# Small transposes and compression layers placed inside projections, output-weight lo's behind P scalings, boundary banks exchanged, in a two-layer hybrid decoder trunk

## Chip, cores and metric

One core of a Trainium2 chip (trn2). The metric is device time in microseconds (us) of one launch, shown as the median of several runs with the lowest and the highest.

## What is computed

The input x has 256 tokens of 1,024 values in float32. Two layers follow each other, each `x <- x + RMSNorm_post(mixer(RMSNorm_pre(x)))`. The first mixer is chunked gated linear attention (GLA). The second is sparse attention (NSA) with three branches per query: compressed, selected and window. Its input projection yields, beside q and a gate z, three pairs of keys and values:

```python
q, kc, vc, ks, vs, kw, vw, gl, z = jnp.split(p, splits, axis=-1)
kc, ks, kw = rope(kc), rope(ks), rope(kw)          # 4 groups x 64
kcmp = compress(kc, pe_k, ck_w1, ck_w2)            # silu(flat(blocks + pe) @ w1) @ w2
vcmp = compress(vc, pe_v, cv_w1, cv_w2)
o = sum over branches of gate * softmax(q k^T) v   # per branch
return (o * silu(z)) @ w_out
```

(The last lines are shortened from the reference.) A result is to be exact to float32, which decides how matrix products are done.

## The kernel before

**Products.** TensorE multiplies rounded float32. Each operand is split into a hi (ScalarE, line 190) and a lo, which is raw minus hi (line 196), made by GpSimd (POOL) or VectorE (DVE) according to a table `LOS`. `mm3` (line 210) then runs three matmuls: hi by hi, lo by hi, hi by lo. Weights come by DMA in units of two k rows (SP's queue, four raw buffers; a raw buffer is free again when hi and lo have been made from it).

**Projections.** `proj` (line 222) runs 8 steps of three matmuls for one token tile t (128 tokens) into one accumulator bank; tag acc has two banks, s three, t two, o one. `chain` (line 217) fixes the order of chained pieces on TensorE. What is not chained is placed by the compiler's scheduler, for each engine, by its own forecast; once placed, the order on an engine is fixed.

**The boundary between the layers.** `out_proj(t)` (line 340) finishes layer 0 for a token tile: two banks, one for each half of the 1,024 outputs. `residual` (line 263) evacuates them one after the other: ScalarE squares a bank, VectorE copies it (`yg`, line 276), then the new x is written (line 281). `pre_T` (line 298) transposes x into `hT`, four transposes to a bank, for each half c.

**The projections of layer 1.** In order: kc(0), ks(0), kc(1), ks(1), kw0(0), kw0(1), kw1(0), kw1(1), then q and z; the number in brackets is the token tile. Behind kc, ks and kw0 a chain follows: ScalarE evacuates values (`vs_sb`, line 859, or `dup`, line 845), VectorE rotates keys (`rope`, lines 823 and 825), GpSimd adds the two products twice over into `dup` (line 832), TensorE transposes `dup` four times (`dup_T`, line 839), and ScalarE and VectorE copy the result into `kcT` (lines 849 and 850) or split it into `kTh` and `kTl`. When both token tiles of kcT are there, VectorE makes eight `flat` additions (line 885), and `hidden(u)`, u from 0 to 3 (line 891), multiplies flat by a quarter of the compression weights. A 32-column transpose of `vecs` (line 815) makes vT, which flat wants. `spread` (line 328) sends the norms' factors over the partitions with two matmuls. None of these small pieces is chained.

**The units.** `unit(g, t)` is attention for group g and tile t: scores (line 1001), P by ScalarE's exponentials, coefficients cf on VectorE (line 1041), scalings of P on GpSimd (line 1045), transposes of P (line 1074), products with v (line 1088), and pcT (line 1096) for the compressed branch. Among the last units of tile 0 the output weights are loaded and split (`ch_o`, lines 1217 to 1219), in steps k of 0, 2, 4, 6 and halves n.

## Time and profile before

| | us |
|---|---|
| median of 3 runs | 304.07 (303.97 to 305.38) |
| profiled execution | 302.72 |
| its span in the profile | 300.8 |
| TensorE busy | 286.6 |
| VectorE busy | 215.3 |
| ScalarE busy | 181.5 |
| GpSimd busy | 167.0 |

The rows below come from the profiled execution; their times count from the start of its span. The share of the time outside the span is 302.72 less 300.8, that is 1.9. Engines are written PE (TensorE), DVE (VectorE), ACT (ScalarE), POOL (GpSimd) and SP (which issues DMAs) in rows.

### The profile page before, as it was taken

The numbers are of one execution on the slowest core, as the hardware profiler recorded it, in microseconds if no ns is written. First come the engines' busy times: TensorE is split into PE (matmuls) and PEld (weight loads), VectorE is DVE, ScalarE is ACT, GpSimd is POOL, SyncE is SP. The second block draws the span as 40 slices with busy tenths as digits, with TensorE's granted clock in tenths as the row PEclk, the third lists the DMA queues.
The fourth block names the chain that finished last, engine by engine and source line by source line (L and its number), as shares of the span: only waits on it lengthen the run. The fifth ranks groups of instructions, "written<-read, shape, count | busy, mean of one in ns | idle before, by whom it ended". The sixth has DMA issues, their size and how long they took to land.

```text
span 300.8 us, 5374 instructions
## 1 busy us (share of the span) xinstructions
PE 286.6 (95%) x1788; PEld 239.7 (80%) x1788; DVE 215.3 (72%) x556; ACT 181.5 (60%) x468; POOL 167.0 (56%) x184
## 2 busy tenths in 40 slices
PE   7999999999999999889979999999997999999991
PEld 7888999999998887668958676899994678676660
DVE  1779569846979877576893536799999858877423
ACT  4896788667754757435534405679967637657301
POOL 1496968984383252927545035897799434172200
PEclk9999999999999999999999999999997799999998
DMA  7997588105677334394745785576144000100001
GB/s 214 403 362 217 151 258 288 56 22 186 204 220 212 92 82 130 64 289 147 195 162 144 274 263 180 190 218 232 42 142 139 2 0 0 71 2 0 2 0 71
DMA packets 28301, 44.57 MB, mean 148 GB/s; under 512 B 2865, under 2 KB 12513, under 8 KB 28274
## 3 DMA queue, kind: packets, MB, share of 16 engines
q1 hardware_dynamic: 28242, 44.23, 46.6%
q8 instruction: 14, 0.23, 0.3%
q14 instruction: 13, 0.11, 0.1%
q10 hardware_dynamic: 32, 0.01, 0.0%
HBM read 43.18 MB, written 1.05 MB: 147 GB/s over the span
## 4 chain that ended last, share of the span: by engine, by line
PE 63%; DVE 13%; issue 9%; POOL 6%; ACT 4%; DMA 3%; SPq 0%; POOLq 0%; DVEq 0%; ACTq 0%
PE acc L211 11%; PE acc L213 11%; PE acc L212 11%; PE s L468 4%; POOL lo L196 3%; PE s L212 3%; PE s L211 3%; PE s L213 3%; DVE lo L196 3%; PE o L894 3%; PE t L1074 3%; PE o L1088 3%; PE s L1001 2%; ACT hi L190 2%; DMA raw<-in_gla_w_in_dram 1%
## 5 line engine op out<-in xcount | busy, mean ns | idle before, releaser
L196 POOL TENSOR_TENSOR lo<-raw,hi 128x512 fp32r<-128x512 f32 (+2 forms) x63 | 82.8, 1334 | 44.4 <-ACT hi L190 44.4
L190 ACT ACTIVATE hi<-raw 128x512 fp32r<-128x512 f32 (+2 forms) x120 | 64.2, 583 | 37.7 <-DMA raw<-in_nsa_w_in_dram 26.6
L196 DVE TENSOR_TENSOR lo<-raw,hi 128x512 fp32r<-128x512 f32 (+2 forms) x57 | 53.6, 963 | 13.4 <-ACT hi L190 13.3
L1045 POOL TENSOR_SCALAR P<-P,cf 128x128 f32<-128x128 f32 (+1 forms) x64 | 29.2, 475 | 30.2 <-DVE cf L1041 14.4
L211 PE MATMUL acc<-hT,hi 128*128 128x256 f32 x160 | 45.2, 283 | 0.1
L212 PE MATMUL acc<-hT,hi 128*128 128x256 f32 x160 | 44.8, 280 | 0.0
L213 PE MATMUL acc<-hT,lo 128*128 128x256 f32 x160 | 44.5, 281 | 0.0
L211 PE MATMUL acc<-hi,hT 128*128 128x512 f32 (+2 forms) x112 | 39.2, 350 | 1.2 <-DVE yg L276 0.8
L213 PE MATMUL acc<-hi,hT 128*128 128x512 f32 (+2 forms) x112 | 38.9, 347 | 0.0
L212 PE MATMUL acc<-lo,hT 128*128 128x512 f32 (+2 forms) x112 | 38.8, 346 | 0.0
L1008 ACT ACTIVATE P<-P,mn 128x128 f32<-128x128 f32 (+1 forms) x64 | 28.4, 445 | 7.2 <-DVE mn L1006 5.9
L211 PEld LDWEIGHTS acc<-hT,hi 128*128 128x128 f32 x160 | 30.1, 188 | 0.4 <-DVE zT L362 0.3
L212 PEld LDWEIGHTS acc<-hT,hi 128*128 128x128 f32 x160 | 30.1, 188 | 0.1
L213 PEld LDWEIGHTS acc<-hT,lo 128*128 128x128 f32 x160 | 29.8, 188 | 0.0
L211 PEld LDWEIGHTS acc<-hi,hT 128*128 128x128 f32 x112 | 21.1, 188 | 5.3 <-ACT yg L269 1.2
L1006 DVE CUSTOM_DVE_ANT_0 P<-s,c 128x128 f32<-128x128 f32 (+1 forms) x64 | 20.6, 347 | 5.3 <-PE s L1001 4.4
L213 PEld LDWEIGHTS acc<-hi,hT 128*128 128x128 f32 x112 | 21.1, 188 | 2.9 <-DVE hT L311 0.4
L212 PEld LDWEIGHTS acc<-lo,hT 128*128 128x128 f32 x112 | 21.1, 188 | 2.0
L1074 PE MATMUL t<-c,P 128*128 128x128 f32 x96 | 17.4, 296 | 2.0 <-ACT pcT L1096 1.9
L440 POOL TENSOR_TENSOR lo<-raw,hi 128x512 fp32r<-128x512 f32 (+1 forms) x9 | 12.3, 1388 | 9.9 <-ACT hi L436 9.8
L1074 PEld LDWEIGHTS t<-c,P 128*128 128x128 f32 x96 | 11.1, 147 | 7.3 <-issue 3.6
L832 POOL TENSOR_TENSOR dup<-rt,rt 128x512 f32<-128x512 f32 x6 | 8.9, 1487 | 11.2 <-DVE rt L825 5.7
(268 smaller groups left out, 676.2 us busy)
## 6 DMA issues: line engine op xcount, KB each, us to landing
raw<-in_nsa_w_in_dram SPq DMA_DIRECT2D x24, 512.0 KB, 4.5
raw<-in_gla_w_in_dram SPq DMA_DIRECT2D x12, 512.0 KB, 6.1
raw<-in_gla_w_out_dram SPq DMA_DIRECT2D x8, 512.0 KB, 4.3
raw<-in_nsa_w_out_dram SPq DMA_DIRECT2D x8, 512.0 KB, 4.2
raw<-in_nsa_w_in_dram SPq DMA_DIRECT2D x8, 280.0 KB, 8.4
raw<-in_gla_w_in_dram SPq DMA_DIRECT2D x6, 344.0 KB, 3.4
home<-in_gla_w_in_dram SPq DMA_DIRECT2D x4, 512.0 KB, 6.7
w<-in_nsa_ck_w_dram SPq DMA_DIRECT2D x4, 512.0 KB, 3.8
```

The source lines that it names most:

```text
L190: m = after(nc.scalar.activation(hi[:, j, :n], raw[:, j, :n], AF.Copy), prev)
L196: eng.tensor_sub(lo[:, j, :n], raw[:, j, :n], f(hi[:, j, :n]))
L211: m = nc.tensor.matmul(o, a[0], b[0], start=start, stop=False, **kw)
L212: nc.tensor.matmul(o, a[0], b[1], start=False, stop=False, **kw)
L213: return m, nc.tensor.matmul(o, a[1], b[0], start=False, stop=stop, **kw)
L440: line(e, eng.tensor_sub(lo[:, j, :n], raw[:, j, :n], f(hi[:, j, :n])))
L468: m = nc.tensor.matmul(o[t][:, :chunk.n], hT[i][:, k, t * P:(t + 1) * P], w[j], start=(k == b == 0), stop=(k == KT - 1 and b == 2))
L894: nc.tensor.matmul(hid_b[kv * 64:(kv + 1) * 64, :CHID], flat[:, j, kv].rearrange("p g c -> p (g c)"), w1[u * 2 + kv][:, j % 4, :], start=( ...
L1006: nc.vector.tensor_tensor_reduce(out=o, in0=src, in1=masks[br], op0=ALU.add, op1=ALU.min, scale=-0.125, scalar=3.0e38, accum_out=self.mn[: ...
L1008: nc.scalar.activation(o, o, AF.Exp, scale=-1.0, bias=self.mn[:, j:j + 1], accum_out=self.sm[:, j:j + 1])
L1045: nc.gpsimd.tensor_scalar(o, o, cf[:, i * 2 + br:i * 2 + br + 1], 1.0, op0=ALU.mult, op1=ALU.mult)
L1074: pe(nc.tensor.transpose(b[:, i * P:(i + 1) * P], self.Pt[i][:, c0:c0 + P], ident))
```

## The change

1. **Output weights.** GpSimd's lo's of the output weights with k of 4 and 6 are put behind the last scaling of unit (3, 0) by a dependence in order.
2. **Banks.** In `out_proj(1)` the first half goes to bank acc and the second to s; before, the first went to s and the second to acc.
3. **Small transposes.** `pre_T(1, c)` is chained between steps of ks(0), at k of 4 and 5. The kc(0) transposes and the one of vecs are chained between ks(0) and kc(1). Those of ks(0) are at step 3 of kc(1), those of kc(1) at step 3 of ks(1), those of ks(1) at step 3 of kw0(0). `dup` has three buffers instead of two.
4. **Compression.** hidden(u) is chained; hidden(0) stands behind kw1(0) and hidden(1) behind kw1(1).

```diff
@@ -182,7 +182,7 @@
                 self.raw.append(raw)
...
-        def split_unit(self, prev=None, pace=None):
+        def split_unit(self, prev=None, pace=None, pool_prev=None):
             n, raw = self.n, self.raw[len(self.u)]
...
@@ -193,13 +193,15 @@
                     if i >= 0:
...
                 eng = nc.gpsimd if len(self.u) * 2 + j in self.pool else nc.vector
-                eng.tensor_sub(lo[:, j, :n], raw[:, j, :n], f(hi[:, j, :n]))
+                x = eng.tensor_sub(lo[:, j, :n], raw[:, j, :n], f(hi[:, j, :n]))
+                if eng is nc.gpsimd:
+                    after(x, pool_prev)
             self.u.append((hi, lo))
...
-        def split(self, pace=None):
+        def split(self, pace=None, pool_prev=None):
             while len(self.u) < len(self.raw):
-                self.split_unit(pace=pace)
+                self.split_unit(pace=pace, pool_prev=pool_prev)
             return self
...
@@ -219,12 +221,15 @@
         after(first, last[0])
...
-    def proj(chunk, hT, t, tag="acc"):
+    def proj(chunk, hT, t, tag="acc", between={}):
...
         for k in range(KT):
+            if k in between:
+                chain(first, b)
+                between[k]()
             a, b = mm3(o[:, :chunk.n], [h[:, k, t * P:(t + 1) * P] for h in hT], chunk.part(k), k == 0, k == KT - 1)
-            first = a if k == 0 else first
+            first = a if k == 0 or k in between else first
             chunk.mm[t * KT + k] = a
...
@@ -300,7 +305,7 @@
         b = bank(tag)
...
             m = nc.tensor.transpose(b[:, k * P:(k + 1) * P], X[:, t, (c * 4 + k) * P:(c * 4 + k + 1) * P], ident)
-            if layer == t == 0:
+            if t == 1:
                 chain(m, m)
...
@@ -339,7 +344,7 @@
...
-        o = [bank("s"), bank("acc" if t else "s")]
+        o = [bank("acc" if t else "s"), bank("s")]
         steps = [(k, n) for k in range(4) for n in range(2)] + [(k, n) for n in range(2) for k in range(4, KT)]
...
@@ -773,10 +778,9 @@
     rs1 = []
...
         out_proj(t, ch_o, oT, gpost)
-        for c in range(2):
-            last_hi = pre_T(t, c, 1, hT, "t")
         if t == 0:
-            ks_after = last_hi
+            for c in range(2):
+                ks_after = pre_T(t, c, 1, hT, "t")
         rs1.append(rms(t)[0])
...
@@ -811,9 +815,6 @@
     flat = cp.tile([P, 16, 2, GROUPS, 16], F32, tag="flat", name="flat")
...
     vT = cp.tile([P, 32], F32, tag="vT", name="vT")
-    b = bank()
-    nc.tensor.transpose(b[:, :32], vecs, ident[:32, :32])
-    nc.vector.tensor_copy(vT, b[:, :32])
...
@@ -828,39 +829,52 @@
         if not twice:
...
             return a
-        r = cp.tile([P, nh, 2, DH], F32, tag="dup", name=nm("dup"), bufs=2)
+        r = cp.tile([P, nh, 2, DH], F32, tag="dup", name=nm("dup"), bufs=3)
         nc.gpsimd.tensor_add(r, *(y.unsqueeze(2).to_broadcast([P, nh, 2, DH]) for y in (a, b)))
...
-    def dup_T(r):
+    def dup_T(r, held=True):
...
         for g in range(GROUPS):
-            nc.tensor.transpose(b[:, g * P:(g + 1) * P], r[:, g].rearrange("p e d -> p (e d)"), ident)
+            m = nc.tensor.transpose(b[:, g * P:(g + 1) * P], r[:, g].rearrange("p e d -> p (e d)"), ident)
+            if held:
+                chain(m, m)
         return b
-    def kc_part(t):
-        o = proj(ch_kc, hT, t)
-        rv = cp.tile([P, GROUPS, 2, DH], F32, tag="dup", name=nm("dup"), bufs=2)
+    def kc_part(t, between={}):
+        o = proj(ch_kc, hT, t, between=between)
+        rv = cp.tile([P, GROUPS, 2, DH], F32, tag="dup", name=nm("dup"), bufs=3)
         nc.scalar.activation(rv, o[:, 256:512].rearrange("p (g d) -> p g d", d=DH).unsqueeze(2)
                              .to_broadcast([P, GROUPS, 2, DH]), AF.Copy, scale=rs1[t])
-        for kv, r in ((0, rope(o[:, :256], 4, t, True)), (1, rv)):
-            bv = dup_T(r).rearrange("p (g n two) -> p g n two", g=GROUPS, two=2)
-            nc.scalar.activation(kcT[:64, kv, :, t * 64:(t + 1) * 64], bv[:64, :, :, 0], AF.Copy)
-            nc.vector.tensor_copy(kcT[64:, kv, :, t * 64:(t + 1) * 64], bv[64:, :, :, 1])
-    def k_T(o, t, c0):
-        b = dup_T(rope(o[:, :256], 4, t, True)).rearrange("p (g n) -> p g n", g=GROUPS)
+        parts = ((0, rope(o[:, :256], 4, t, True)), (1, rv))
+        def rest():
+            for kv, r in parts:
+                bv = dup_T(r).rearrange("p (g n two) -> p g n two", g=GROUPS, two=2)
+                nc.scalar.activation(kcT[:64, kv, :, t * 64:(t + 1) * 64], bv[:64, :, :, 0], AF.Copy)
+                nc.vector.tensor_copy(kcT[64:, kv, :, t * 64:(t + 1) * 64], bv[64:, :, :, 1])
+        return rest
+    def k_T(r, c0, held):
+        b = dup_T(r, held).rearrange("p (g n) -> p g n", g=GROUPS)
         split_bank(b, kTh[:, :, c0:c0 + P], kTl[:, :, c0:c0 + P])
-    def ks_part(t):
-        o = proj(ch_ks, hT, t)
+    def ks_part(t, between={}):
+        o = proj(ch_ks, hT, t, between=between)
         nc.scalar.activation(vs_sb[:, t, :], o[:, 256:512], AF.Copy, scale=rs1[t])
-        k_T(o, t, (1 - t) * P)
-    kc_part(0)
-    ks_part(0)
+        r = rope(o[:, :256], 4, t, True)
+        return lambda: k_T(r, (1 - t) * P, True)
+    rest = kc_part(0)
+    ks_rest = ks_part(0, {4 + c: lambda c=c: pre_T(1, c, 1, hT, "t") for c in range(2)})
+    rest()
+    b = bank()
+    m = nc.tensor.transpose(b[:, :32], vecs, ident[:32, :32])
+    chain(m, m)
+    nc.vector.tensor_copy(vT, b[:, :32])
...
@@ -877,29 +891,29 @@
     ch_z = [Chunk(w_in, N_Z + p * 512, 512) for p in range(2)]
...
     ch_kw[0].load()
-    kc_part(1)
+    rest = kc_part(1, {3: ks_rest})
+    ks_rest = ks_part(1, {3: rest})
     for kv in range(2):
...
                                  vT[:, kv * 16:(kv + 1) * 16].unsqueeze(2).to_broadcast([P, 16, NCMP]))
-    ks_part(1)
     hid_b = bank("o")
...
             for kv in range(2):
-                nc.tensor.matmul(hid_b[kv * 64:(kv + 1) * 64, :CHID], flat[:, j, kv].rearrange("p g c -> p (g c)"),
-                                 w1[u * 2 + kv][:, j % 4, :], start=(j == 0), stop=(j == 15))
+                m = nc.tensor.matmul(hid_b[kv * 64:(kv + 1) * 64, :CHID], flat[:, j, kv].rearrange("p g c -> p (g c)"),
+                                     w1[u * 2 + kv][:, j % 4, :], start=(j == 0), stop=(j == 15))
+                chain(m, m)
...
     for t in range(NT):
-        o = proj(ch_kw[0], hT, t)
+        o = proj(ch_kw[0], hT, t, between={3: ks_rest} if t == 0 else {})
         nc.scalar.activation(vw_sb[:, t, :24], o[:, 256:280], AF.Copy, scale=rs1[t])
-        k_T(o, t, 272 + t * P)
-    hidden(0)
+        k_T(rope(o[:, :256], 4, t, True), 272 + t * P, False)
     ch_kw[1].load().split((ch_kw[0], PA[7]))
...
@@ -911,7 +925,7 @@
         nc.scalar.activation(g, g, AF.Exp, scale=-1.0)
...
         nc.vector.reciprocal(g, g)
-    hidden(1)
+        hidden(t)
...
@@ -1042,7 +1056,8 @@
             for br in range(2):
...
                     o = self.Pt[2 * h + i][:, br * n:(br + 1) * n]
-                    nc.gpsimd.tensor_scalar(o, o, cf[:, i * 2 + br:i * 2 + br + 1], 1.0, op0=ALU.mult, op1=ALU.mult)
+                    self.scaled = nc.gpsimd.tensor_scalar(o, o, cf[:, i * 2 + br:i * 2 + br + 1], 1.0, op0=ALU.mult,
+                                                          op1=ALU.mult)
...
@@ -1216,7 +1231,7 @@
         U[g, 0].finish()
...
         for n in range(2):
-            ch_o[n].load(k, k + 2).split((ch_z[1], k + 2 * n + PA[12]))
+            ch_o[n].load(k, k + 2).split((ch_z[1], k + 2 * n + PA[12]), U[3, 0].scaled if k >= 4 else None)
     run(out_steps(0))
...
```

The number of instructions stays. How the scheduler orders the engines with it is shown at three places; a name's number tells tiles apart and differs between the two programs.

TensorE in projection kw0. Before, in kw0(1) (its bank is acc_1870), between its steps 4 and 5:

```order
L211 MATMUL acc_1870<-hi_1818,hT_1317 128x280
L212 MATMUL acc_1870<-lo_1819,hT_1317 128x280
L213 MATMUL acc_1870<-hi_1818,hT_1318 128x280
L839 MATMUL t_1787<-c_64,dup_1785 128x128 [waits DVE_49,Pool_49]
L839 MATMUL t_1787<-c_64,dup_1785 128x128 x3
L337 MATMUL t_1795<-dg_1799,onesr 128x256 [waits DVE_49]
L337 MATMUL t_1795<-dg_1800,onesr 128x256
L211 MATMUL acc_1870<-hi_1818,hT_1317 128x280
L212 MATMUL acc_1870<-lo_1819,hT_1317 128x280
```

Of the change, in kw0(0) (its bank is acc_1823), around its step 2:

```order
L215 MATMUL acc_1823<-hi_1799,hT_1318 128x280
L213 MATMUL acc_1823<-hi_1805,hT_1317 128x280 [waits Activation_49]
L214 MATMUL acc_1823<-lo_1806,hT_1317 128x280 [waits Pool_49]
L215 MATMUL acc_1823<-hi_1805,hT_1318 128x280
L342 MATMUL t_1788<-dg_1792,onesr 128x256 [waits DVE_49]
L342 MATMUL t_1788<-dg_1793,onesr 128x256
L840 MATMUL t_1833<-c_64,dup_1777 128x128 [waits Pool_49]
L840 MATMUL t_1833<-c_64,dup_1777 128x128 x3
L213 MATMUL acc_1823<-hi_1805,hT_1317 128x280
```

The transposes of ks(1) (dup_1785, now dup_1777) moved from the second token tile of kw0 to the third step of the first, behind the spread matmuls.

VectorE at the same place. Before, from the rotation of ks(1) (bank acc_1754) on:

```order
L823 TENSOR_TENSOR rt_306_1780<-acc_1754,cos_t 128x256 [waits Activation_49]
L825 TENSOR_TENSOR rt_307_1781<-acc_1754,sin_t 128x4x32 [waits Pool_49]
L825 TENSOR_TENSOR rt_307_1781<-acc_1754,sin_t 128x4x32
L196 TENSOR_TENSOR lo_1927<-raw_1918,hi_1926 128x280 [waits Activation_49]
L196 TENSOR_TENSOR lo_1933<-raw_1920,hi_1932 128x280 [waits DMAHW7_49,Activation_49]
L196 TENSOR_TENSOR lo_1933<-raw_1920,hi_1932 128x280 [waits Activation_49]
L196 TENSOR_TENSOR lo_1939<-raw_1922,hi_1938 128x280 [waits DMAHW0_49,Activation_49]
L850 COPY kcT<-t_1732 64x4x64 [waits Activation_49]
L850 COPY kcT<-t_1739 64x4x64 [waits Activation_49]
L885 TENSOR_TENSOR flat<-kcT,vT 128x16x15 [waits DVE_49]
L885 TENSOR_TENSOR flat<-kcT,vT 128x16x15 x3
L196 TENSOR_TENSOR lo_1945<-raw_1924,hi_1944 128x280 [waits DMAHW1_49,Activation_49]
```

Of the change (the bank of ks(1) is acc_1732):

```order
L196 TENSOR_TENSOR lo_1806<-raw_1685,hi_1805 128x280 [waits DMAHW3_49,Activation_49]
L196 TENSOR_TENSOR lo_1818<-raw_1689,hi_1817 128x280 [waits DMAHW5_49,Activation_49]
L857 COPY kcT<-t_1742 64x4x64 [waits Activation_49]
L857 COPY kcT<-t_1749 64x4x64 [waits Activation_49]
L900 TENSOR_TENSOR flat<-kcT,vT 128x16x15 [waits DVE_49]
L900 TENSOR_TENSOR flat<-kcT,vT 128x16x15 x3
L900 TENSOR_TENSOR flat<-kcT,vT 128x16x15 [waits DVE_49]
L900 TENSOR_TENSOR flat<-kcT,vT 128x16x15 x3
L824 TENSOR_TENSOR rt_306_1772<-acc_1732,cos_t 128x256 [waits Activation_49]
L826 TENSOR_TENSOR rt_307_1773<-acc_1732,sin_t 128x4x32 [waits Pool_49]
L826 TENSOR_TENSOR rt_307_1773<-acc_1732,sin_t 128x4x32
L343 COPY rb<-t_1788 128x256 [waits PE_49]
```

The rotation of ks(1) stood ahead of the kcT copies and the flat additions; it now stands behind all of them.

GpSimd among the last units of the first token tile; P_2845 and P_2868 are of unit (3, 0), P_3064 of unit (0, 1), lo_2967, lo_2975 and lo_2983 of the output weights. Before:

```order
L196 TENSOR_TENSOR lo_2967<-raw_2964,hi_2966 128x512 [waits Activation_49]
L196 TENSOR_TENSOR lo_2975<-raw_2972,hi_2974 128x512 [waits PE_49,DMAHW5_49,Activation_49,Pool_49]
L196 TENSOR_TENSOR lo_2983<-raw_2980,hi_2982 128x512 [waits DMAHW6_49,PE_49,Activation_49]
L196 TENSOR_TENSOR lo_2983<-raw_2980,hi_2982 128x512 [waits Activation_49]
L1045 TENSOR_SCALAR P_2845<-P_2845,cf_2844 128x128 [waits DVE_49,Activation_49]
L1045 TENSOR_SCALAR P_2845<-P_2845,cf_2844 128x128 [waits Activation_49]
L1045 TENSOR_SCALAR P_2845<-P_2845,cf_2844 128x128
L1045 TENSOR_SCALAR P_2845<-P_2845,cf_2844 128x128 [waits Activation_49]
L1045 TENSOR_SCALAR P_2868<-P_2868,cf_2844 128x128 [waits DVE_49,Activation_49]
L1045 TENSOR_SCALAR P_2868<-P_2868,cf_2844 128x128 [waits Activation_49]
L1045 TENSOR_SCALAR P_2868<-P_2868,cf_2844 128x128
L1045 TENSOR_SCALAR P_2868<-P_2868,cf_2844 128x128 [waits Activation_49]
```

Of the change:

```order
L1059 TENSOR_SCALAR P_2868<-P_2868,cf_2844 128x128 [waits Activation_49]
L1059 TENSOR_SCALAR P_2868<-P_2868,cf_2844 128x128
L1059 TENSOR_SCALAR P_2868<-P_2868,cf_2844 128x128 [waits Activation_49]
L196 TENSOR_TENSOR lo_2967<-raw_2964,hi_2966 128x512 [waits DMAHW4_49,PE_49,Pool_49]
L196 TENSOR_TENSOR lo_2967<-raw_2964,hi_2966 128x512
L196 TENSOR_TENSOR lo_2975<-raw_2972,hi_2974 128x512 [waits DMAHW5_49,PE_49,Pool_49]
L196 TENSOR_TENSOR lo_2983<-raw_2980,hi_2982 128x512 [waits DMAHW6_49,PE_49,Pool_49]
L196 TENSOR_TENSOR lo_2983<-raw_2980,hi_2982 128x512
L1059 TENSOR_SCALAR P_3064<-P_3064,cf_3063 128x256 [waits DVE_49,Activation_49]
```

Five lo's moved from ahead of the scalings of P_2845 and P_2868 to behind them, and so to right ahead of those of P_3064.

## Rows read from the trace of the kernel before

**Rows 1.** The head of the profile page: the span, and TensorE's busy time, its share of the span and its instructions.

```profile
span 300.8 us, 5374 instructions
...
PE 286.6 (95%) x1788; PEld 239.7 (80%) x1788; DVE 215.3 (72%) x556; ACT 181.5 (60%) x468; POOL 167.0 (56%) x184
```

**Rows 2.** Waits of TensorE (PE) over the whole span: the bank it wanted to write and the line, what it waited for, us in total, how many waits, the longest.

```profile
PE t L1074 <- ACT pcT L1096: 1.9, 2, 1.8
PE o L894 <- DVE flat L885: 1.6, 1, 1.6
...
PE acc L211 <- DVE yg L276: 0.8, 1, 0.8
PE t L815 <- DVE xg L307: 0.7, 1, 0.7
...
PE acc L211 <- ACT hT L310: 0.4, 1, 0.4
```

**Rows 3.** Windows: stretch, its length, then busy us (and instructions) of PE, its weight loads, DVE (VectorE), ACT (ScalarE) and POOL (GpSimd), then the granted TensorE clock, the DMA share and GB/s.

```profile
152.00:154.00 2.00, 0.52 (x6) 0.38 (x8) 1.97 (x6) 0.87 (x2) 0.00 (x0) 1.00 0.73 208
227.00:229.00 2.00, 1.22 (x9) 0.47 (x7) 2.00 (x10) 1.22 (x3) 2.00 (x6) 1.00 0.71 214
230.00:236.00 6.00, 6.00 (x24) 4.36 (x26) 6.00 (x15) 3.92 (x13) 3.42 (x3) 0.50 0.00 1
```

**Rows 4.** The chain of waits between 215 and 232 us, in order of time: start, us, what.

```profile
222.84 1.26 POOL lo L196
...
224.12 3.58 DMA raw<-in_nsa_w_out_dram
...
230.00 1.09 PE t L1074 x4
```

**Rows 5.** Timeline at the start of the boundary, VectorE and TensorE: start, us, engine, line, operation, out<-in, partitions x elements, how many in the row, and in brackets the idle time ahead and what ended it.

```profile
121.02 0.68 DVE L276 SCALAR_TENSOR_TENSOR yg<-s,gpost 128x512 f32<-128x512 f32 x1
...
121.69 0.68 DVE L276 SCALAR_TENSOR_TENSOR yg<-acc,gpost 128x512 f32<-128x512 f32 x1
...
122.51 0.47 PE L211 MATMUL acc<-hi,hT 128*128 128x512 f32 x1 [0.76 <-DVE yg L276]
```

**Rows 6.** Timeline of TensorE where kc(1) ends, and of VectorE where it writes the second token tile of x back; columns as in Rows 5.

```profile
124.76 1.42 DVE L281 SCALAR_TENSOR_TENSOR x_sb<-yg,ss,x_sb 128x512 f32<-128x512 f32 x2 [0.73 <-POOL ss L275]
...
137.63 0.60 PE L839 MATMUL t<-c,dup 128*128 128x128 f32 x4
137.99 0.48 PE L212 MATMUL acc<-lo,hT 128*128 128x512 f32 x1
138.31 0.40 PE L213 MATMUL acc<-hi,hT 128*128 128x512 f32 x1
138.54 0.39 PE L211 MATMUL acc<-hi,hT 128*128 128x512 f32 x1
```

**Rows 7.** Timeline of the chain that prepares small transposes, ScalarE, VectorE and GpSimd; columns as in Rows 5.

```profile
137.66 0.69 ACT L845 ACTIVATE dup<-acc,rs_r 128x512 f32<-128x512 f32 x1 [0.32 <-PE acc L213]
...
138.38 0.42 DVE L823 TENSOR_TENSOR rt<-acc,cos_t 128x256 f32<-128x256 f32 x1 [1.31 <-ACT dup L845]
138.72 0.48 DVE L825 TENSOR_TENSOR rt<-acc,sin_t 128x128 f32<-128x128 f32 x2
...
139.83 1.50 POOL L832 TENSOR_TENSOR dup<-rt,rt 128x512 f32<-128x512 f32 x1
...
143.64 0.47 ACT L859 ACTIVATE vs_sb<-acc,rs_r 128x256 f32<-128x256 f32 x1 [2.56 <-PE acc L213]
...
148.13 0.77 DVE L850 COPY kcT<-t 64x256 f32<-64x256 f32 x2
```

**Rows 8.** Timeline of VectorE and GpSimd: lo's on either engine, and the flat additions; columns as in Rows 5.

```profile
136.62 0.45 DVE L196 TENSOR_TENSOR lo<-raw,hi 128x280 fp32r<-128x280 f32 x1 [2.12 <-ACT hi L190]
...
136.99 1.54 POOL L196 TENSOR_TENSOR lo<-raw,hi 128x280 fp32r<-128x280 f32 x2 [3.24 <-ACT hi L190]
...
140.70 1.89 DVE L196 TENSOR_TENSOR lo<-raw,hi 128x280 fp32r<-128x280 f32 x2
...
141.29 1.95 POOL L196 TENSOR_TENSOR lo<-raw,hi 128x280 fp32r<-128x280 f32 x2
...
148.93 2.18 DVE L885 TENSOR_TENSOR flat<-kcT,vT 128x240 f32<-128x240 f32 x4
...
151.40 2.02 DVE L885 TENSOR_TENSOR flat<-kcT,vT 128x240 f32<-128x240 f32 x4
```

**Rows 9.** Timeline of TensorE: matmuls of the compression layer, the long run and one visit between the matmuls of q; columns as in Rows 5.

```profile
153.48 2.81 PE L894 MATMUL o<-w,flat 128*64 128x256 f32 x24 [1.57 <-DVE flat L885]
...
170.26 0.65 PE L894 MATMUL o<-w,flat 128*64 128x256 f32 x2
```

**Rows 10.** Timeline of GpSimd and TensorE among the last units of the first token tile; columns as in Rows 5.

```profile
228.47 4.94 POOL L196 TENSOR_TENSOR lo<-raw,hi 128x512 fp32r<-128x512 f32 x4
...
239.35 2.35 POOL L1045 TENSOR_SCALAR P<-P,cf 128x128 f32<-128x128 f32 x4 [1.37 <-DVE cf L1041]
242.04 1.91 POOL L1045 TENSOR_SCALAR P<-P,cf 128x256 f32<-128x256 f32 x4 [0.34 <-DVE cf L1041]
...
226.75 0.66 PE L1074 MATMUL t<-c,P 128*128 128x128 f32 x4
...
249.88 0.29 PE L1001 MATMUL s<-kTl,qS 128*128 128x272 f32 x1
```

## The prediction

> **What bounds the kernel now.** I read the page first: TensorE is busy for 286.6 of a span of 300.8 us [rows 1]. Its queue is the path almost everywhere, and what an edit is worth is the time for which that queue stands still. So the waits of TensorE came second [rows 2]: these five make 5.4 us, and four of them lie in the stretch that the change rewrites, from 121 to 154 us; the longest lies near 230. Third came windows [rows 3]: the granted clock is 1.00 (2.4 GHz) through the pause of 1.6 for flat between 152 and 154, and it stands at 0.50 (1.2 GHz) from 230 to 236, behind the pause of 1.8. Fourth came the chain of waits ahead of 230 [rows 4], to see what that longest wait hangs on. Last I laid the order of the changed program over the timeline of the boundary, engine by engine. Times below are on the clock of the profile of before, in us; a hand-over from one engine to the next costs 0.14 (122.37 to 122.51 in [rows 5]).
>
> **The boundary's start.** VectorE copies bank s at 121.02 and acc at 121.69 (0.68 each), and ks(0), which wants the acc bank, starts at 122.51 [rows 5]. With acc as the first of the two, it starts 0.14 after the first copy: 121.83, that is 0.68 earlier.
>
> **The second token tile's transposes, inside ks(0).** A matmul 128x512 takes 0.23 (138.31 to 138.54), so a step of three takes 0.70; four transposes take 0.36 (137.63 to 137.99), and the first matmul after a break 0.09 more [rows 6]. TensorE is at step 4 by 121.83 + 0.09 + 2.80 = 124.7. What it must transpose is written by two instructions from 124.76 on, 0.71 each [rows 6]; the first half is there at 125.6. A **new wait of 0.9**. The second half is there in time. ks(0) ends at 125.6 + 0.45 + 0.70 + 0.45 + 2.10 = 129.3.
>
> **The transposes between ks(0) and kc(1).** Eight of kc last until 130.0. The 32-column one behind them wants a transpose bank, which VectorE frees by its kcT copy (0.39). In the changed order that copy stands behind the rotation of ks(0) (0.82), which waits for ScalarE's vs_sb (0.47): 129.3 + 0.47 + 0.82 + 0.39 + 0.14 = 131.1 [rows 7]. A **new wait of 1.1**. kc(1) starts at 131.3 and, with four transposes at its step 3, ends at 131.3 + 0.09 + 5.60 + 0.45 = 137.5. Before, the same work was done at 137.76, which is 137.99 [rows 6] less one matmul of ks(1) that had run by then. So 0.68 and the old waits of 0.7 and 0.4 [rows 2] are given back by 0.9 and 1.1, and this part is **0.25 ahead** (0.6 ahead to 0.3 behind, with or without three hand-overs).
>
> **The kc transposes inside ks(1).** TensorE is at step 3 by 137.5 + 0.09 + 2.10 = 139.7. Its input goes through ScalarE's dup (0.69), the rotation (0.82) and GpSimd's dup (1.50) [rows 7]: ready at 140.6. In the old order these transposes came a projection later, and nothing waited. **Wait 0.9** (0.6 to 1.2). ks(1) ends at 140.6 + 0.72 + 0.09 + 3.50 = 144.9.
>
> **The ks transposes inside kw0(0).** By the widths against 128x512, the two spread matmuls take 0.23 and nine matmuls of 280 columns 1.15; with two breaks TensorE is at step 3 by 146.5. The transposes wait for a rotation that now stands on VectorE behind two kcT copies (0.77) and the eight flat additions (2.18 + 2.02) [rows 7, 8]; before, the rotation came ahead of them. Copies from 141.6, flats from 142.4 to 146.6, rotation to 147.4, dup to 148.9: a wait of 2.4 with nothing in the way. But behind its dup of kc GpSimd works off five weight lo's of kw0, at 0.77 each from 140.6 to 144.4, so the first flats run beside two or three of them. The nearest rows for two-input additions on both engines at once are the pairs at 140.70 and 141.29: 0.95 each beside 0.98, against 0.45 and 0.77 where they run apart [rows 8]. Over some 2.1 us VectorE thus runs at half its pace and loses 1.1. Bounds: nothing (2.4) and a turn for every lo left (2.8 at 0.77, 2.2 more: 4.6). I take **3.5**, since the pairs are the same kind of instruction.
>
> *SBUF — State Buffer* of the Trainium skill (Who interferes with whom) has it that a VectorE instruction with two SBUF inputs and a GpSimd instruction that reads SBUF shut each other out for as long as one lasts; that speaks against flats beside lo's. By that rule the wait would be 4.6 and the sum 1.1 more. The trace bears it out in part: taking turns, each VectorE addition at 140.70 would have lost a whole lo of 0.77, and it lost 0.50.
>
> **What goes with it.** The wait of 1.6 for flat [rows 2] ends, since hidden(0) now stands behind kw1(0). The compression matmuls break into projections five times instead of seven; a visit of two takes 0.65 where two of the long run take 0.23 [rows 9], so two visits fewer save 0.8 (0.4 to 1.0). Their weight loads move in SP's queue, but none behind a wait that ends later than the step it feeds. The boundary comes to -0.25 + 0.9 + 3.5 - 1.6 - 0.8 = **+1.8** (-0.2 to +4.1).
>
> **The scalings ahead of lo's.** On GpSimd P_2647 moves ahead of one lo, P_2845 and P_2868 ahead of five. The wait at 230.0 does not hang on them: its chain runs from the lo at 222.84 through a weight transfer of 3.58, the hi, the exponentials and pcT [rows 4], and all of these keep their places. From there to 250 TensorE waits for nothing, so scalings that end earlier are worth nothing. Late next are P_3064's scalings, now behind the five lo's. P_2868's end at 239.35 + 2.35 = 241.7; five lo's at 1.24 end at 247.9; four scalings (1.91) at 249.8 [rows 10]. TensorE reaches their transposes, which moved behind s_3211, at 249.88 + 0.12, less 0.4 for the four that now follow: 249.6. Wait 0 to 0.9 (the upper end with lo's slowed by VectorE's, as in [rows 8]), taken as **0.3**. The moved lo's themselves are wanted after that, and the first is done by 244.2.
>
> **Sum.** +1.8 + 0.3 = +2.1. The profiled execution took 302.72, 1.35 below the median of the three runs, 304.07. Profiled 304.8, median **306.2**.
>
> **The rivals.**
> *A, faster.* VectorE loses two lo's near 225 and 232, and its small steps meet fewer of GpSimd's, so that the pause before 230 closes and the clock stays up. For it: additions beside lo's run at half their pace [rows 8]. Against: no VectorE step is in the chain of [rows 4]. Price: four transposes take 1.09 at 0.50 [rows 4] and 0.66 at 1.00 [rows 10], so 0.39 of 6.6 us, 2.6; and 1.8 for the pause: 306.2 - 4.4 = **301.8**.
> *B, slower still.* The pause of 3.5 in kw0(0) brings the clock to 0.50, as that of 1.8 did. For it: no pause before was as long. Against: the pause of 1.6 left it at 1.00, and around the new one projections run without a gap, while TensorE had worked for only 1.22 of the 2 us to 229 [rows 3]. [...] The same 2.6: **308.8**.
> *C, no change.* VectorE and GpSimd run ahead of my chains and the four new waits of the boundary (6.4) come out at half: 306.2 - 3.2 = **303.0**. For it: they are hand-over times added up, and each error adds too. Against: every link is a measured row.
> *L, slower too.* VectorE and GpSimd take turns in kw0(0), a whole lo for each flat while lo's are left: +1.1, **307.3**. For and against it: the half-pace pairs [rows 8], which lie between.
>
> **How the numbers follow.** A measurement of this kernel tells 0.5% (1.5 us) from no change: faster is below 302.55, slower above 305.59. The forecast has 0.32, with a range of its own from 304.5 to 307.5 (0.11 of the 0.32 within 0.5%); A 0.18, C 0.20 (0.08 of it faster, 0.12 no change), B 0.22, L 0.08. Faster 0.26, same 0.23, slower 0.51. The range, 301.6 to 309.0, runs from just under A's time to just over B's and leaves out half of either.
>
> **What would show it.** Among TensorE's waits none for yg of 0.8, none for xg or flat; instead one for x_sb near 125, one for a kcT copy near 130, one for GpSimd's dup near 140, and the boundary's longest for a dup between 146 and 150. ks(0) starting at 121.8. The wait for pcT still 1.8, with the clock at 0.50 behind it. I am wrong if the wait in kw0(0) is under 2, if the clock falls behind it, or if the pause at 230 has gone.

## The result, and the profile after

Times are medians over all runs; ratios and their intervals leave out disturbed executions.

| | before | after |
|---|---|---|
| median, us | 304.07 | 307.95 (305.02 to 311.31) |
| ratio to before | | 1.0102 [1.0074, 1.013] |
| profiled execution | 302.72 | 307.67 |
| its span | 300.8 | 305.7 |

The change is slower by 0.7 to 1.3%. The lines that answer to those of before, with the same columns. First the head of the page, beside [rows 1]:

```profile
span 305.7 us, 5370 instructions
...
PE 286.4 (94%) x1788; PEld 241.0 (79%) x1788; DVE 217.0 (71%) x556; ACT 181.3 (59%) x468; POOL 167.0 (55%) x184
```

TensorE's busy time is 0.2 less than before, so the longer span is time in which it stands still, on balance: what matmuls take longer at half clock counts as busy, and the compression layer's fewer visits make up for it. VectorE, ScalarE and GpSimd run as many instructions as before; of all kinds there are four fewer. TensorE's waits, beside [rows 2]:

```profile
PE t L840 <- POOL dup L833: 5.0, 2, 3.6
PE t L1089 <- ACT pcT L1111: 3.0, 2, 2.9
PE t L875 <- DVE kcT L857: 1.7, 1, 1.7
...
PE t L307 <- DVE x_sb L286: 0.8, 1, 0.8
...
PE t L1089 <- POOL P L1059: 0.4, 1, 0.4
```

yg, xg, hT and flat are gone, and the five waits foretold stand in their place. TensorE's timeline where it waits, then where it runs the compression layer among the matmuls of q, beside [rows 5, 6, 9]:

```profile
125.52 0.63 PE L307 MATMUL t<-c,x_sb 128*128 128x128 f32 x4 [0.79 <-DVE x_sb L286]
...
131.96 0.24 PE L875 MATMUL t<-c,vecs 32*128 32x32 f32 x1 [1.69 <-DVE kcT L857]
...
141.87 0.33 PE L840 MATMUL t<-c,dup 128*128 128x128 f32 x1 [1.32 <-POOL dup L833]
...
151.50 0.84 PE L840 MATMUL t<-c,dup 128*128 128x128 f32 x4 [3.63 <-POOL dup L833]
...
175.73 1.95 PE L908 MATMUL o<-w,flat 128*64 128x256 f32 x16
...
254.59 0.44 PE L1089 MATMUL t<-c,P 128*128 128x128 f32 x2 [0.43 <-POOL P L1059]
```

VectorE and GpSimd ahead of the wait of 3.63, beside [rows 7, 8]:

```profile
141.78 4.45 POOL L196 TENSOR_TENSOR lo<-raw,hi 128x280 fp32r<-128x280 f32 x5
...
143.87 5.33 DVE L900 TENSOR_TENSOR flat<-kcT,vT 128x240 f32<-128x240 f32 x8
149.22 0.42 DVE L824 TENSOR_TENSOR rt<-acc,cos_t 128x256 f32<-128x256 f32 x1
...
150.18 1.26 POOL L833 TENSOR_TENSOR dup<-rt,rt 128x512 f32<-128x512 f32 x1 [3.96 <-DVE rt L826]
```

The eight flats, part of them beside the lo's, take 5.33 (4.20 before), and the rotation that the transposes hang on starts behind the last of them. Windows behind that wait, and behind the one for pcT (columns as in [rows 3]):

```profile
152.00:154.00 2.00, 2.00 (x10) 2.00 (x9) 2.00 (x4) 0.92 (x2) 1.34 (x2) 0.50 0.15 15
154.00:156.00 2.00, 2.00 (x13) 2.00 (x13) 1.34 (x5) 0.28 (x1) 0.00 (x0) 0.69 0.87 249
...
234.00:240.00 6.00, 5.31 (x22) 4.03 (x22) 1.96 (x9) 4.36 (x17) 0.98 (x3) 0.50 0.01 1
```

The clock is at 0.50 (1.2 GHz) behind both; before, behind the second alone. The chain to the wait for pcT, beside [rows 4]:

```profile
226.76 1.27 POOL lo L196
...
228.04 4.35 DMA raw<-in_nsa_w_out_dram
...
234.69 1.09 PE t L1089 x4
```

**Where the 4.95 went** (the profiled executions took 302.72 and 307.67). I call *boundary* the stretch from VectorE's first copy for yg (121.02 before [rows 5], 120.87 after) to q's first matmul (164.46, 169.94): the same work lies in it. Before:

```profile
164.46 0.50 PE L211 MATMUL acc<-hi,hT 128*128 128x512 f32 x1
```

After:

```profile
120.87 0.68 DVE L281 SCALAR_TENSOR_TENSOR yg<-acc,gpost 128x512 f32<-128x512 f32 x1
...
169.94 0.50 PE L213 MATMUL acc<-hi,hT 128*128 128x512 f32 x1
```

It went from 43.44 to 49.07, +5.63. ks(0) starts 0.67 earlier behind that copy; the new waits are 0.79 + 1.69 + 1.32 + 3.63 = 7.43; the old ones, 0.71 + 0.42 + 1.57 = 2.70, are gone; that leaves 1.57, which I put down to the half clock behind the longest wait. From q on it is 0.53 shorter: 32 compression matmuls took 4.90 and take 3.75, the projections that they broke into 0.41 less; the wait for pcT is 1.09 longer, that for P 0.43 new; the rest, -0.49, I can't place. With the start, -0.15, that makes 4.95.

### The profile page after: what moved, and what is told of

Read it like the earlier page. It is cut to its first block, busy times and chain, and to the rows that moved or that the text cites. A ratio compares the mean times of both kernels' runs of the same rounds, so it can differ in the third digit from the quotient of the medians.

```text
span 305.7 us, 5370 instructions
## 1 busy us (share of the span) xinstructions
PE 286.4 (94%) x1788; PEld 241.0 (79%) x1788; DVE 217.0 (71%) x556; ACT 181.3 (59%) x468; POOL 167.0 (55%) x184
## 3 DMA queue, kind: packets, MB, share of 16 engines
HBM read 43.18 MB, written 1.05 MB: 145 GB/s over the span
## 4 chain that ended last, share of the span: by engine, by line
PE 59%; DVE 12%; POOL 10%; issue 9%; ACT 4%; DMA 3%; SPq 0%; POOLq 0%; DVEq 0%; ACTq 0%
PE acc L213 10%; PE acc L214 10%; PE acc L215 10%; POOL lo L196 5%; PE s L473 4%; PE s L213 3%; PE s L214 3%; PE s L215 3%; PE t L1089 3%; PE o L908 3%; POOL P L1059 2%; DVE lo L196 2%; PE o L1103 2%; DVE flat L900 2%; PE s L1015 2%
## 5 line engine op out<-in xcount | busy, mean ns | idle before, releaser
L1059 POOL TENSOR_SCALAR P<-P,cf 128x128 f32<-128x128 f32 (+1 forms) x64 | 30.0, 489 | 30.9 <-DVE cf L1055 10.0
L213 PE MATMUL acc<-hi,hT 128*128 128x512 f32 (+2 forms) x112 | 40.4, 361 | 0.2
L215 PE MATMUL acc<-hi,hT 128*128 128x512 f32 (+2 forms) x112 | 39.3, 350 | 0.0
L213 PEld LDWEIGHTS acc<-hi,hT 128*128 128x128 f32 x112 | 21.8, 195 | 4.0 <-issue 0.8
L215 PEld LDWEIGHTS acc<-hi,hT 128*128 128x128 f32 x112 | 21.6, 193 | 2.6 <-DVE hT L316 0.4
L214 PEld LDWEIGHTS acc<-lo,hT 128*128 128x128 f32 x112 | 21.8, 195 | 1.8
L833 POOL TENSOR_TENSOR dup<-rt,rt 128x512 f32<-128x512 f32 x6 | 8.0, 1327 | 19.8 <-DVE rt L826 12.3
```

Source lines behind the costliest of these rows:

```text
L213: m = nc.tensor.matmul(o, a[0], b[0], start=start, stop=False, **kw)
L214: nc.tensor.matmul(o, a[0], b[1], start=False, stop=False, **kw)
L215: return m, nc.tensor.matmul(o, a[1], b[0], start=False, stop=stop, **kw)
L1059: self.scaled = nc.gpsimd.tensor_scalar(o, o, cf[:, i * 2 + br:i * 2 + br + 1], 1.0, op0=ALU.mult, op1=ALU.mult)
```

## The experiments

The boundary's length is the measure where a few us hang on one stretch, since the whole time also moves with what the units do behind it. The median and ratio are against the kernel before on the same chip.

| | boundary | waits of TensorE in it | median | ratio |
|---|---|---|---|---|
| before | 43.44 | yg .76, xg .71, hT .42, flat 1.57 | | |
| change | 49.07 | x_sb .79, vecs 1.69, dup 1.32 and 3.63 | 307.95 | 1.0102 [1.0074, 1.013] |
| e1 | 50.43 | as the change, but dup 1.60, then rt 2.77 | 309.14 | 1.0144 [1.0075, 1.0212] |
| e2 | 47.69 | as the change, but dup 0.83 | 307.87 | 1.0108 [1.0028, 1.0188] |
| e3 | 43.42 | as before | 303.34 | 0.9964 [0.9921, 1.0006] |
| e4 | 46.14 | as the change, but vecs 0.28 | 307.71 | 1.0107 [1.0071, 1.0143] |
| e5 | 45.39 | x_sb .78, rt 2.87 | 305.01 | 1.0023 [0.9992, 1.0055] |
| e6 | 46.86 | yg .76, xg .72, hT .41, hi 3.14 | 305.25 | 1.0021 [0.9987, 1.0055] |
| e7 | 43.44 | as before | 304.2 | 1.002 [0.9983, 1.0058] |
| e8 | 46.65 | x_sb .8, rt 3.1 | 305.4 | 1.002 [0.9983, 1.0057] |
| e9 | 42.35 | x_sb .79, flat 1.63 | 301.56 | 0.9905 [0.9868, 0.9942] |
| e10 | 50.73 | x_sb .76, vecs 1.73, dup 1.34 and 3.66 | 309.94 | 1.0165 [1.011, 1.0221] |
| e11 | 45.55 | as the change, but dup 1.64 | 303.6 | 0.9978 [0.9946, 1.001] |
| e12 | 42.23 | x_sb .78, flat 1.19 | 301.49 | 0.9915 [0.9883, 0.9947] |

**First round: are the waits what they seem, and is each worth its length?** e1 puts the flats behind the rotation of ks(1); `rot[0]` is that rotation's last product.

```diff
-            nc.vector.tensor_add(flat[:, :, kv, g, :NCMP], src,
+            x = nc.vector.tensor_add(flat[:, :, kv, g, :NCMP], src,
...
+            after(x, rot[0])
```

> The changed kernel with one order more on VectorE: the eight flat additions stand behind the rotation of ks(1). Theory 1 (the time went into small transposes that stand in TensorE's queue before their input is ready, above all those of ks(1) in kw0(0)): the rotation starts when vs_sb is there, near 147.0, dup is done near 149.1, and TensorE waits about 1.4 us there instead of 3.6; no stretch at half clock behind it; about 3.6 us less than the changed kernel, so 303 to 304.5. Theory 2 (the pause in kw0(0) hides behind something that comes later anyway, such as the weight transfers ahead of 230 us): the wait shrinks and the time stays above 306.

Theory 1 fell: the wait shrank to 1.60, but the time, 309.14, stayed above 306 as Theory 2 has it, if not for the transfers that it names. A wait of 2.77 came at the start of kw1(0), for the rotation of kw0(0), which frees its bank and now stood behind flats and lo's:

```profile
149.68 0.66 PE L842 MATMUL t<-c,dup 128*128 128x128 f32 x4 [1.60 <-POOL dup L835]
158.11 0.48 PE L213 MATMUL acc<-hi,hT 128*128 128x280 f32 x1 [2.77 <-DVE rt L828]
```

A wait that VectorE's order makes was not removed but moved. e2 fills the wait in kw0(0) with matmuls whose product nobody reads.

```diff
+            for i in range(23):
+                m = nc.tensor.matmul(bd[:, :280], hT[0][:, 0, :P], ch_kw[0].part(0)[0], start=True, stop=True)
+                chain(m, m)
             ks_rest()
```

> The changed kernel with 23 matmuls of 280 columns (about 3 us at full clock), whose product nobody reads, put into TensorE's queue ahead of the ks transposes in kw0(0). The transposes can start no earlier, so the wait's own 3.6 us are still lost; only the clock's part can come back. Theory 1a (the pause lowers the clock, and the half-clock stretch behind it, 3.4 us long, costs about 1.4 us): granted clock 1.00 throughout 150 to 156, 1.0 to 1.7 us less than the changed kernel. Theory 1b (that stretch hides under other waits, or the clock falls in any case): within 0.5 us of the changed kernel.

The clock stayed at 1.00 and the boundary is 1.38 shorter, near the 1.57 put down to the half clock; the total could not be told apart. e3 is the kernel before with part 1 alone.

> The kernel before with the order of the output-weight lo's alone (part 1 of the change). Theory 1: nothing gained, since no scaling is in the chain ahead of 230 us; 0 to 0.5 us slower by a new wait for the scaling of P_3064 near 250: 304.0 to 304.6, and the pause ahead of 230 stays at 1.8 us. Theory 3 (this part made that pause longer, 2.9 us in the changed kernel, and the stretch at half clock with it): 1 us slower or more, with the pause near 2.9. Theory A (the small steps of VectorE are freed and the pause closes): 2 us faster or more.

The boundary is untouched, the wait for P is there (0.4), and the total is not longer: part 1 is not what costs. e4 is the change with the vecs transpose ahead of kc(0)'s.

```diff
-    rest()
     b = bank()
     m = nc.tensor.transpose(b[:, :32], vecs, ident[:32, :32])
...
+    rest()
```

> The changed kernel with the 32-column transpose of vecs ahead of the kc(0) transposes instead of behind them. Theory 1: the wait of 1.7 us for the bank that the kcT copy frees falls to 0.3 to 0.7 (for the copy of vT), and the time to about 1.1 us under the changed kernel, since everything behind it hangs on TensorE's own progress. Theory 2 (later waits swallow it): the wait for GpSimd's dup near 140 or that in kw0(0) grows by as much, and the time stays.

In the profiled execution TensorE was 1.4 ahead at the wait in kw0(0), which stayed as long (3.62): this time its chain starts from TensorE's own work, so the gain was kept up to q. And the clock did not fall behind it:

```profile
150.00:156.00 6.00, 5.77 (x46) 5.77 (x47) 4.79 (x10) 1.28 (x4) 3.14 (x4) 1.00 0.54 151
```

Those two, 1.41 and 1.57, are 2.98, against the 2.93 between 49.07 and 46.14. The whole time does not show the gain: the ratio to before is 1.0107, and 1.0102 for the change. The profiled execution was the fastest of ten (306.18, mean granted clock 0.985); the other nine have mean clocks of 0.972 to 0.978, so the clock of the profiled one does not stand for them.

**Second round: parts undone or alone.** e5 no longer chains the small K transposes and that of vecs (the last line below).

```diff
-    def dup_T(r, held=True):
+    def dup_T(r, held=False):
...
-        return lambda: k_T(r, (1 - t) * P, True)
+        return lambda: k_T(r, (1 - t) * P, False)
...
-    chain(m, m)
```

> The changed kernel, but the small K transposes (of kc, ks, kw0) and the one of vecs are not chained any more: the scheduler places them, as it did before the change. Kept are the exchanged banks, the second token tile's transposes of x inside ks(0), the chained compression layer and the lo's behind the scalings. In its order the transposes of kc(1) stand at step 3 of kw0(0) and those of ks(1) at step 5 of kw0(1), and VectorE's rotation of ks(1) stands ahead of the flat additions, as before. Theory 1 (the time is lost in waits for transposes held too early): the waits of 1.69 for vecs, 1.32 and 3.63 for GpSimd's dup go, that for x_sb of 0.8 stays, and the waits of before for yg (0.7 of it), xg 0.7, hT 0.4 and flat 1.6 stay away. Against the profiled 302.7 of before: -0.7 -0.7 -0.4 -1.6 +0.8, some -0.5 for fewer visits of the compression layer: -3.1, so 300 to 301 in the median, and no fall of the clock between 145 and 160. Theory 2 (the other parts cost something too, the banks or the chained compression layer above all): between 302.5 and 305.

Theory 1 fell (305.01, where it had 300 to 301). Three of the waits went, but one of 2.87 came at the start of kw1(0). It hangs on VectorE; the chain of waits reads (start, us, what):

```profile
147.48 2.46 DVE flat L899 x4
149.95 0.36 DVE lo L196
150.31 1.95 DVE flat L899 x4
152.27 0.42 DVE rt L824
...
153.24 0.37 PE acc L213
```

e6 is the kernel before with part 4 alone: hidden chained, hidden(t) behind kw1(t).

```diff
+                chain(m, m)
...
-    hidden(0)
...
-    hidden(1)
+        hidden(t)
```

> The kernel before with part 4 alone: the compression layer chained behind kw1(0) and kw1(1). Theory 1: the wait of 1.6 for flat goes and the visits between other matmuls save 0.4 to 1.0; everything ahead of 150 as before: 301.5 to 302.3 in the median, ratio 0.992 to 0.995. Rival: the wait was cover for VectorE, which is full from 150 to 160, so a projection behind it waits for about as long (1 to 1.6 on a hi, lo or bank before 165): 303.5 to 304.

The rival holds in the boundary, at twice its size: instead of 1.57 for flat, 3.14 for a hi at the start of kw1(0), half clock behind it, and a boundary 3.42 longer. The ratio, 1.0021 [0.9987, 1.0055], does not tell the whole time from before. Its chain of waits:

```profile
145.65 2.87 DVE lo L196 x3
148.58 4.91 DMA raw<-in_nsa_w_in_dram
153.59 1.16 ACT hi L190 x2
...
154.88 0.45 PE acc L211
```

This chain runs through VectorE's lo's, which free the raw buffers, and a weight transfer, and not through the flats. But VectorE's rotation of kw0(0), which stands behind all eight flats and frees the bank that kw1(0) writes, ended in the same moment (154.26 + 0.48 = 154.74, the hi's at 153.59 + 1.16 = 154.75):

```profile
153.91 0.42 DVE L823 TENSOR_TENSOR rt<-acc,cos_t 128x256 f32<-128x256 f32 x1
154.26 0.48 DVE L825 TENSOR_TENSOR rt<-acc,sin_t 128x128 f32<-128x128 f32 x2
```

So either alone would have held kw1(0) until then. Before, the wait for flat and 26 compression matmuls lay between kw0(1) and kw1(0), and kw1(0) began at 156.22 with everything at hand (beside [rows 9]):

```profile
151.26 0.65 PE L894 MATMUL o<-w,flat 128*64 128x256 f32 x2
...
156.22 0.40 PE L211 MATMUL acc<-hi,hT 128*128 128x280 f32 x1
```

e7 and e8 put 14 matmuls into the pause ahead of 230, in the kernel before and in that of e5.

```diff
+    bd, m = bank("acc"), U[1, 0].tc
+    for _ in range(14):
+        m = after(nc.tensor.matmul(bd[:, :272], U[2, 0].q[0], kTh[:, 2, P:400], start=True, stop=True), m)
```

> The kernel before with 14 matmuls of 272 columns added (into a free accumulator bank, nobody reads it) in the pause ahead of 230, between the transpose for pcT of one unit and the transposes of P of the next. They put nothing into the chain of waits there, so the pause for the lo, the weight and pcT is as long as it was; only TensorE has work in it. Theory 1 (the pause lets the clock fall, and that costs 2.4 to 2.6 in the 6 us behind it): granted clock 1.00 from 228 to 240, and 301.3 to 302 in the median. Rival 1 (the clock falls for another cause than the pause): 0.50 from 230 to 236 as before, 304. Rival 2 (the clock stays up, but the stretch behind the pause then waits for VectorE and GpSimd, which work at their own pace): clock 1.00, new waits of TensorE of 1 to 2 us between 231 and 240, 303 to 304.

> The kernel with the small transposes not chained, and the 14 added matmuls in the pause ahead of 230. If both gains are real and independent, their sum: about 298 to 299 in the median, clock 1.00 over the whole span. If the pause is 4.4 long with a transfer of 4.35, the added matmuls (some 1.7 us) fill it only in part, and the clock may fall all the same: 300 to 301.

In e7 the wait for pcT was filled, and TensorE stood still 5 us later instead, with the clock at 0.50 behind that:

```profile
228.61 2.00 PE L1220 MATMUL acc<-kTh,qS 128*128 128x272 f32 x14
...
236.04 0.65 PE L1092 MATMUL o<-pT,vs_sb 128*64 128x256 f32 x4 [1.81 <-DVE of L356]
```

That is its second rival, with a fall of the clock that it did not have. Of e7's twelve executions seven kept a mean granted clock of 0.991 or more and took 302.7 to 304.6, five had 0.983 to 0.985 and took 305.9 to 306.9; the median, 304.2, gains nothing on before. e8 says nothing on this: in e5, e6, e8, e9 and e12 the scheduler lays the last units in another order, in which no such pause stands near 230; instead there is one of 1.8 to 1.9 for cS between 204 and 210.

**Third round: a theory that fits.** From 144 to 154 VectorE has a fixed amount to do (lo's of kw0, kcT copies, eight flats, rotations), and TensorE did not get past kw1(0)'s start without it in e1, e5 or e6, whatever stood first. The compression layer at its old place was the work that lay over that time. Move it away, or stop TensorE ahead of it with held transposes, and TensorE stands for some 3 us. e9 is e5 with the compression layer at its old place; e10 is the whole change with it there. hidden(0) and 5 of the 8 instructions of hidden(1) (each is two matmuls in the profile) stand behind kw0(1), as in the kernel before, the other 3 behind kw1(1).

```diff
+    hidden(0)
...
+    hidden(1, range(5))
...
-        hidden(t)
+    hidden(1, range(5, 8))
```

> The changed kernel with the small K transposes and that of vecs not chained, and the compression layer back at its old place: 13 of its instructions between kw0(1) and kw1(0), 3 behind kw1(1). Of the change there remain the exchanged banks, the second tile's transposes of x inside ks(0), and the lo's behind the scalings. Length of the boundary, from VectorE's first copy for yg to the first matmul of q (the same work lies between): 43.4 before, 49.1 with the whole change, 45.4 without the chained transposes, 46.9 with the compression layer's move alone. New theory (VectorE's work from 144 to 154 sets when TensorE can go on; the compression layer used to fill that time, and with it gone or with transposes held ahead of it TensorE stands): no wait of about 3 before kw1(0), the wait for flat of 1.6 is back, boundary 42.2 to 42.8; 302.5 to 303.5 in the median, or 300.5 to 301.5 if the clock stays up near 230. Old theory (the place of the compression layer costs nothing, 1.6 for flat was its price): boundary above 45.

> The changed kernel, all transposes chained as in it, but the compression layer at its old place (13 instructions between kw0(1) and kw1(0), 3 behind kw1(1)). New theory: the held transposes in kw0(0) stop TensorE ahead of the compression layer, so its place no longer matters: the wait of 3.6 stays, no wait for flat, boundary 48 to 49.5 and 307 to 308.5. Rival (each part has its own price, 3.4 for the compression layer's move, 2 for the held transposes): boundary 45 to 46.5, 304 to 305.

The waits of both came out by the new theory; e10's boundary (50.73) and time lie above their ranges. e9 has no wait at kw1(0), flat is back, and its boundary is 1.09 shorter than before:

```profile
126.09 0.63 PE L307 MATMUL t<-c,x_sb 128*128 128x128 f32 x4 [0.79 <-DVE x_sb L286]
150.53 0.65 PE L909 MATMUL o<-w,flat 128*64 128x256 f32 x2
152.81 2.81 PE L909 MATMUL o<-w,flat 128*64 128x256 f32 x24 [1.63 <-DVE flat L899]
```

In e10 the held transposes wait as in the change, and the place of the layer is worth nothing. That it is 1.66 longer still is a second fall of the clock, behind the wait for vecs, which in the change's own profile it survived:

```profile
134.00:138.00 4.00, 4.00 (x15) 3.24 (x14) 0.59 (x1) 0.93 (x2) 0.00 (x0) 0.61 0.91 310
```

e11 takes work off VectorE in the whole change, by the first two lines; e12 has GpSimd make three of e9's flats, by the last.

```diff
-    for kv in range(2):
+    for kv in range(1):
...
+            eng = nc.gpsimd if kv * GROUPS + g >= 5 else nc.vector
```

> The changed kernel with four of the eight flat additions left out (those of the values; the products with them then see zeros), so VectorE has 2.7 less to do between the kcT copies and the rotation of ks(1). New theory (VectorE's work sets the wait): the wait in kw0(0) falls from 3.6 to 0.9 or 1.0, the clock stays at 1.00 there, no new wait before 170, boundary 49.1 - 2.7 - 1.5 = 44.9 (46.4 if the clock falls all the same), 303.5 to 305. Rival 1 (the weight transfers of kw1 are as late): a new wait for a hi of 1 to 2.5 before kw1(0), boundary 46.5 to 48. Rival 2 (GpSimd's lo's set it, through its dup): the wait falls by 1 or less.

> The version of the compression layer's old place with free transposes, and three of the eight flat additions made by GpSimd, which stands idle there for some 5 us. New theory: VectorE ends its backlog earlier; the wait for flat of 1.6 falls to 0.5 to 0.9 (GpSimd's additions run beside VectorE's at half pace), boundary 41.3 to 42; median 0.7 to 1 below that version, so 301.5 to 302.5, 299.5 to 300.5 if the clock stays up near 230. Rival (two engines on the same memory gain nothing): wait 1.6, no difference to that version.

In e11 VectorE's four flats took 3.35, three of them beside GpSimd's last lo's:

```profile
142.87 3.54 POOL L196 TENSOR_TENSOR lo<-raw,hi 128x280 fp32r<-128x280 f32 x4
...
144.00 3.35 DVE L900 TENSOR_TENSOR flat<-kcT,vT 128x240 f32<-128x240 f32 x4
```

So 5.33 - 3.35 = 1.98 was saved, and the wait fell by 1.99, to 1.64. It did not fall to 0.9 or 1.0, since the four flats that are left are the longer half: the first four of the change took 3.31 of its 5.33. The clock stayed up, and 1.99 + 1.57 is 3.56, against the 3.52 by which the boundary shrank. No new wait came there. So less work for VectorE shortens the wait by as much. In e12, sharing gained 0.18 of the wait (1.19, and 0.26 of issue, time in which TensorE waited for nothing that the profile shows, for 1.63), and the time is that of e9 (301.49 for 301.56), as the rival has it. The additions on both engines took longer than alone:

```profile
148.22 3.34 DVE L900 TENSOR_TENSOR flat<-kcT,vT 128x240 f32<-128x240 f32 x4
...
148.29 2.92 POOL L900 TENSOR_TENSOR flat<-kcT,vT 128x240 f32<-128x240 f32 x3
```

e9 beats both kernels. Its profiled execution is 1.09 shorter than that of before (301.63 for 302.72), as much as its boundary; its median is 2.0 below. What lies behind q was not taken apart: the last units stand in another order, with the clock at 1.00 from 230 to 236, and the compression layer breaks in three times for four. A gain from that order would be luck as far as the change is concerned. Neither the exchanged banks nor the second tile's transposes, which e5, e9 and e12 keep, were run alone.

## Why the prediction was right, and where it was not

The direction and the waits by name and place were right. The median, 307.95, lies within the range, but above the 304.5 to 307.5 of the forecast itself. Rival B came in addition: by the prediction's own sign, "if the clock falls behind it", the forecast without B does not stand. The sum holds partly because misses cancel.

- **Boundary's start**: 0.68 forecast, 0.67. **x_sb**: 0.9, came as 0.79.
- **vecs**: 1.1, came as 1.69. The chain of [rows 7] was right, but VectorE also had the second tile's lo's of hT and small steps of the norm ahead of the rotation, which began at 130.63. The two numbers for this stretch, up to the end of kc(1), do not agree: 0.68 + 0.7 + 0.4 against 0.9 + 1.1 is 0.22 behind and not 0.25 ahead (the new waits are counted from where the next matmul could have started, the old ones, as in rows, from where the last one ended). It came out 0.68 behind (0.67 + 0.71 + 0.42 against 0.79 + 1.69).
- **dup in ks(1)**: 0.9, came as 1.32 (above its bound of 1.2).
- **dup in kw0(0)**: 3.5, came as 3.63, and by the steps given: 5.33 for the flats against 4.20 + 1.1. VectorE beside GpSimd is slowed by 1.13 in all, as the pairs of [rows 8] had it (1.1). Whole turns (rival L) would have made the wait 4.6 by the prediction's sum.
- **What goes with it**: here a step failed. "The wait of 1.6 for flat [rows 2] ends, since hidden(0) now stands behind kw1(0)": it ended, but not for that reason. In e10 hidden(0) is back at its old place and the wait is gone all the same, since the held transposes stop TensorE until VectorE is past the flats. Without held transposes (e6) the move turns 1.57 for flat into 3.14 at kw1(0) and makes the boundary 3.42 longer: the wait was where TensorE met VectorE's backlog, and the matmuls behind it covered what kw1(0) needs. The booked 1.6 came out right only because the price of the move and that of the dup wait are one, not two.
- **Hidden visits**: 0.8, came as 1.15 + 0.41, from q on and not in the boundary.
- **Wait for P_3064**: 0.3, came as 0.43. **The wait for pcT** was to stay at 1.8 and came as 2.88; the weight transfer in its chain took 4.35 for 3.58. Part 1 alone is not the cause (e3: 2.06). The transfer's length does not settle it either: waits of 2.88 go with 4.35, 4.37 (e1) and 4.32 (e10), one of 2.22 with 3.51 (e2), but 2.06 with 4.67 (e3) and 2.08 with 5.31 (e11). The cause stays open.
- **Rival B** came in addition: the clock fell behind the wait in kw0(0), for 1.57 and not 2.6. To weigh a fall behind the forecast wait was right, but the length of a wait does not settle it: the same wait of 3.6 left the clock up in e4's profiled execution.

Summed over the profiled execution, +2.1 was forecast and +4.95 measured. The larger part of the difference is the clock (1.57), the wait for pcT (1.09), the stretch up to the end of kc(1) (0.68 behind for 0.25 ahead, 0.93) and dup (0.42), less 0.76 for visits and the 0.49 that I can't place.

## What to carry over

In these runs a wait on a full engine was that engine's backlog seen from TensorE: reordering moved it (e1, e5, e6), and less work for that engine (e11) or TensorE work laid over it (e9) made it shorter. Before moving work away from a wait, ask what the wait and that work were covering together; the next consumer behind them pays. Price two edits that stop the same queue on the same backlog once, and test them crossed (e5, e6, e9, e10), since alone each looked like a loss of its own.

## What was not expected of the hardware

- **The clock's fall is not settled by the pause.** At the wait of 3.6 in kw0(0) the granted clock fell in the profiled executions of the change and of e10 and stayed at 1.00 in that of e4; near 230 it fell behind 1.79 [rows 2, 3] and stayed up behind 2.06 in e3 and 2.08 in e11; behind 1.83 to 1.94 for cS it fell in e5, e6, e8 and e12 and not in e9. *TensorE: Matmul & The Clock Gate* of the Trainium skill (Part 1) says that the moment of a transition (the rise, there) differs from run to run of one kernel. Executions of one kernel here differ in their mean granted clock: three of e3's ten have 0.998 and took 300.6 to 301.1, seven have 0.983 to 0.988 and took 303.0 to 304.1, so some 2.7 lie between the two groups. Among those of the change are 305.0 and 305.6 at 0.992, 306.7 to 307.3 at 0.983 and 0.984, and 307.7, as profiled, at 0.977.
- **VectorE beside GpSimd.** Flats beside GpSimd's lo's took 0.78 to 1.08 each in the change and in e11, against 0.56 to 0.61 alone in the kernel before; a lo took 1.03 to 1.05 beside flats and 0.79 and 0.80 apart from VectorE's additions in the kernel before [rows 8]. In e12 GpSimd's own flats took 0.93 to 1.10, and VectorE's beside them 0.63 to 1.02. *SBUF — State Buffer* of the Trainium skill (Who interferes with whom) has one engine shut out for a whole instruction of the other. By that I would estimate 0.56 + 0.79 = 1.35 for a flat; the runs show both slowed, and neither by a whole turn. From the change, a flat beside lo's, one behind them, and a lo beside flats:

```profile
144.57 1.06 DVE L900 TENSOR_TENSOR flat<-kcT,vT 128x240 f32<-128x240 f32 x1
...
148.15 0.56 DVE L900 TENSOR_TENSOR flat<-kcT,vT 128x240 f32<-128x240 f32 x1
...
144.22 1.03 POOL L196 TENSOR_TENSOR lo<-raw,hi 128x280 fp32r<-128x280 f32 x1
```
